# Silu and gating of the attention's four pairs of heads: in the attention's own gate units, or in the output stage

## The chip, the cores and the metric

One core of one Trainium2 chip. The metric is the device time of one launch in microseconds (us); each kernel is run several times and the median is taken. The profile is of one execution.

## What is computed

One layer of a backbone: 1024 tokens of width 1024 and 256 context tokens. A modulated RMS norm gives h; one projection gives eight groups of 512 columns; half of them feed a neighbourhood attention with 8 heads of 64, half a gated short convolution. Each branch is multiplied by the silu of its own gate column group, and one output projection and the residual follow. In the reference:

```python
q, k, v, za, u, bg, cg, zc = jnp.split(h @ w_in, SPLIT_POINTS, axis=-1)
attn = neighbourhood_attention(q, k, heads(v), kc, vc, rpb) * jax.nn.silu(za)
conv = gated_short_conv(u, bg, cg, zc, conv_w, conv_b)
x_new = x + gate[:, None] * (jnp.concatenate([attn, conv], axis=-1) @ w_out)
```

The change concerns the factor silu(za) and the division by the softmax's sums: attn = o * (1/sum) * silu(z), element by element, where o is the product of exponentials and v before it is divided.

## The kernel before, in words

Data stand with features on the 128 partitions and tokens along the free axis. Two heads make a pair: rows 0 to 63 are one head, rows 64 to 127 the other, so there are four pairs (NPAIR), numbered f = 0 to 3. The concatenated input of the output projection has eight such row blocks: 0 to 3 are the attention's pairs, 4 to 7 the convolution's groups. Every float32 product is made of three matmuls of high and low halves (`mm3`, lines 72 to 77).

There are four stages: (1) the norm and modulation of h, with the first convolution group; (2) the projections to q, k and v, which are stored to DRAM head by head; (3) the attention; (4) the output projection. What the change touches lies at the end of stage 2, in stage 3 and in stage 4.

**Stage 3** runs `quarter(n)` (line 1057) for n from 0 to 35: four quarters a head, and a pipeline over three of them (scores of quarter n, exponentials of quarter n-2, products with v of quarter n-3). Between these, on PE, run fillers: the remaining projections, one *unit* each (`unit`, line 338: 128 columns of w_in times all of h, in two halves of 512 tokens, 24 matmuls a half into PSUM tile `pu`, of which there are two). The fillers are first the four gate units of the attention (`attn_group(f)`, line 484), then the units of convolution groups 1 to 3 (`conv_group`, line 384). TICKS (line 33) says how many filler steps each quarter takes. PE, ACT, DVE and POOL run their instructions in the order in which this code writes them; transfers are placed by a scheduler that works with its own estimates of times.

What follows a unit on ACT and DVE is put into a list by `chore` (line 301); `do_acts` (line 307), at the end of each quarter, writes ACT's part. For a gate unit of the attention this is `silus` (line 477): both halves are put through silu from PSUM into `zs` (SBUF), and stored by SP's queue into DRAM tile `zs_d[f]`. The exponentials of the same stage need another table of ACT than silu does, so a table is loaded on either side.

At the end of each head, `finish` (line 1029) copies o and the sums (`ob`) and stores them from ACT's queue, `o_d` and `rs_d`. When a pair is done, `gated(p)` (line 1257) is started for pairs 0 to 2. It is a generator, and each quarter takes one step of it: load the sums, take reciprocals on DVE, store them (`ri_d`); then, for each half, load `zs` and `tb` (from o_d) and the reciprocals `rb` spread over 64 partitions each (`load_sums`, line 505, two transfers), all from SP's queue; multiply `zs` by `rb` on DVE; multiply `tb` by that on DVE and store it to `y_d[f]`. For pair 3 only the reciprocals are made (`recip`, line 498, from POOL's queue).

**Stage 4** takes the eight row blocks in the order FORDER = 4, 5, 6, 0, 1, 2, 3, 7. `put_y(f)` (line 1324) loads both halves of a block's y (tile `tb`, tag `zt`, four buffers, from ACT's queue), writes the high part on ACT (`yh`) and the low part on DVE (`yl`). For pair 3 it loads z's silu and o in place of y, the reciprocals from POOL's queue (tag `rb`, two buffers), and does the two multiplies on DVE there. `load_wo` (line 1315) loads and splits 128 rows of the output weights, one of two halves of 512 columns (`woraw`, two buffers; `woh` on ACT, `wol` on DVE). PE first runs all eight blocks through the first six of eight token tiles of the first half (the *first pass*), then the remaining ten tiles one after the other, 24 matmuls each. `out_tile` (line 1360) multiplies by the gate (DVE), adds x (POOL) and stores. In this stage no order is written by hand: the scheduler orders every engine's instructions by its own estimates.

The functions in full:

Of the kernel before, what the change touches and what calls it, by code (L numbers as in the profile page):

```python
# [10 lines left out]
F32 = mybir.dt.float32  # L11
F32R = mybir.dt.float32r
BF16 = mybir.dt.bfloat16
AF = mybir.ActivationFunctionType
ALU = mybir.AluOpType
# [4 lines left out]
P = 128  # L20
D = 1024
T = 1024
# [5 lines left out]
NPAIR = NH // 2  # L28
# [11 lines left out]
def body(tc, es, x, ctxt, w_ada, b_ada, w_in, q_g, k_g, rpbr, w_out, vecs, cst, out):  # L40
# [21 lines left out]
    pe, act, dve, pool = every = [ordered(e) for e in (nc.tensor, nc.scalar, nc.vector, nc.gpsimd)]  # L62
    sp = ordered(nc.sync)

    def sbuf(name, side=None, bufs=1):
        kw = {} if side is None else {"side": side}
        return tc.tile_pool(name=name, bufs=bufs, reuse_waits="tile", **kw)

    def psum(name):
        return tc.tile_pool(name=name, bufs=1, space=PSUM, reuse_waits="tile")  # L70
# [19 lines left out]
    def many(name, n, shape):  # L90
        return [dr.tile(shape, F32, name=f"{name}{i}")[:] for i in range(n)]
# [4 lines left out]
    o_d = many("o_d", NPAIR, [P, T])  # L96
    y_d = many("y_d", KT, [P, T])
    g_d = dr.tile([1, D], F32, name="g_d")
    rope_d = dr.tile([P, 2048], F32, name="rope_d")
    rs_d = many("rs_d", NPAIR, [2, 2, 512])  # L100
    zs_d = many("zs_d", NPAIR, [P, T])


    q_d = many("q_d", NH, [2, HD, 4, 2, 256])
# [46 lines left out]
    cvp = hs.enter_context(sbuf("cvp", side="right"))  # L151
# [149 lines left out]
    def chore(on_act=None, on_dve=None, queue=soon, frees=None):  # L301
        queue.append([on_act, on_dve, frees])
        if act not in strict:
            do_acts()
            do_dves()

    def do_acts():
        for c in soon + (slow if not any(c[1] and c[1].__name__ == "product" for c in soon) else []):
            if c[0]:
                c[0]()  # L310
                c[0] = None

    def do_dves(most=99):
        for queue in chores:
            while queue and not queue[0][0] and (queue is soon or most > 0 and not soon):
                on_dve = queue.pop(0)[1]
                if on_dve:
                    on_dve()
                    most -= 1
# [18 lines left out]
    def unit(col):  # L338

        w = ahead.pop(col, None)  # L340
        if w is None:
            w = []
            for r in loaded.pop(col, None) or unit_load(col):
                unit_split(r, w)
        nxt = follows.get(col)
        for half in range(2):
            cols = slice(half * 512, (half + 1) * 512)
            for k in range(KT):
                if k % 2 == 0:
                    yield None  # L350
                if k == 0:
                    while any(c[2] == half for c in slow):
                        do_acts()
                        do_dves()
                    ps = psm.tile([P, 512], F32, name="pu", tag="U", bufs=2)
                if k % 2 == 0:
                    tick = 4 * half + k // 2
                    if nxt and tick == 0:
                        raws = unit_load(nxt)
                    if nxt and tick in (3, 5):  # L360
                        unit_split(raws[tick // 5], ahead.setdefault(nxt, []))
                mm3(ps, *w[k], hh[k][:, cols], hl[k][:, cols], k == 0, k == KT - 1)
            yield half, ps

    def blocked(v):
        return v.rearrange("p (b r c) -> p b r c", b=4, r=16)
# [14 lines left out]
    def z_col(f):  # L381
        return CZA + f * P if f < 4 else CZC + (f - 4) * P
# [94 lines left out]
    def silus(z):  # L477
        out = []
        for half, ps in z:
            out.append(cvp.tile([P, 512], F32, name="zs", tag="ub", bufs=2))  # L480
            act.activation(out[half], ps, AF.Silu)
        return out

    def attn_group(f):

        z = []
        for got in unit(z_col(f)):
            if got:
                z.append(got)
            else:  # L490
                yield

        def on_act():
            for half, zs in enumerate(silus(z)):
                sp.dma_start(zs_d[f][:, half * 512:(half + 1) * 512], zs)
        chore(on_act)

    def recip(p, pl):

        ri = pl.tile([P, 16], F32, name="ri", tag="ri", bufs=4)  # L500
        pool.dma_start(ri, rs_d[p].rearrange("h b (x c) -> (h b x) c", c=16))
        dve.reciprocal(ri, ri)
        pool.dma_start(ri_d[p].rearrange("h (x c) -> (h x) c", c=16), ri)

    def load_sums(f, half, rb, queue):
        for i in range(2):
            queue.dma_start(rb[64 * i:64 * i + 64],
                            ri_d[f][i:i + 1, half * 512:(half + 1) * 512].broadcast_to([64, 512]))
# [390 lines left out]
    class gate_row:  # L899
# [7 lines left out]
        def load(self, kt):  # L907
            at, tag = ((bmp, "kc_s"), (uw, "uraw"))[kt % 2]
            self.w[kt] = [at.tile([P, 512], F32, name="gs", tag=tag, bufs=2) for _ in range(2)]
            for nh in range(2):  # L910
                sp.dma_start(self.w[kt][nh], w_ada[0, kt * P:(kt + 1) * P, 2 * D + nh * 512:2 * D + (nh + 1) * 512])
# [249 lines left out]
    for n in range(NT + 3):  # L1161


        p, t = divmod(n, NB)
# [89 lines left out]

    gating = []

    def gated(f):

        ri = ap.tile([P, 16], F32, name="ri", tag="ri", bufs=4)
        sp.dma_start(ri, rs_d[f].rearrange("h b (x c) -> (h b x) c", c=16))  # L1260
        yield
        dve.reciprocal(ri, ri)
        sp.dma_start(ri_d[f].rearrange("h (x c) -> (h x) c", c=16), ri)
        yield
        for half in range(2):
            cols = slice(half * 512, (half + 1) * 512)
            zs, tb, rb = (ap.tile([P, 512], F32, name=n, tag=n, bufs=1) for n in ("zs", "tb", "rb"))
            sp.dma_start(zs, zs_d[f][:, cols])
            sp.dma_start(tb, o_d[f][:, cols])
            load_sums(f, half, rb, sp)  # L1270
            yield
            dve.tensor_tensor(zs, zs, rb, ALU.mult)
            yield
            dve.tensor_tensor(tb, tb, zs, ALU.mult)
            sp.dma_start(y_d[f][:, cols], tb)

    with sbuf("att") as ap, psum("psb") as psb:
        sbank = psb.tile([P, 2, 512], F32, name="pss")
        strict[:] = every
        mx = ap.tile([P, T], F32, name="mx")  # L1280
        sb_new = lambda: ap.tile([P, 2, 384], F32, name="sb", tag="sb", bufs=3)
        mg = ap.tile([P, T], F32, name="mg")
        heads[0].load_v()
        for n in range(4 * NH + 4):
            h, g = divmod(n, 4)
            if 0 < h < NH and g == 0:
                heads[h].load_v()
            if h + 1 < NH and g:
                nx = heads[h + 1]
                for load in ((nx.masks, nx.load_q), (nx.load_k,), ())[g - 1]:  # L1290
                    load()
            quarter(n)
            if ready:
                p = ready.pop()
                if p < NPAIR - 1:
                    gating[:] = [gated(p)]
                else:
                    recip(p, ap)
        for _ in fill:
            do_dves()  # L1300
            do_acts()
        while soon or slow:
            do_dves()
            do_acts()
        strict[:] = []
# [5 lines left out]
    op = es.enter_context(sbuf("op"))  # L1311
# [12 lines left out]
    def put_y(yp, f):  # L1324

        yh = yp.tile([P, T], F32R, name=f"yh{f}")
        yl = yp.tile([P, T], F32R, name=f"yl{f}")
        for half in range(2):
            cols = slice(half * 512, (half + 1) * 512)
            tb = op.tile([P, 512], F32, name="tb", tag="zt", bufs=4)  # L1330
            if f == NPAIR - 1:
                zs = op.tile([P, 512], F32, name="zs", tag="zt", bufs=4)
                rb = op.tile([P, 512], F32, name="rb", tag="rb", bufs=2)
                act.dma_start(zs, zs_d[f][:, cols])
                act.dma_start(tb, o_d[f][:, cols])
                load_sums(f, half, rb, pool)
                dve.tensor_tensor(zs, zs, rb, ALU.mult)
                dve.tensor_tensor(tb, tb, zs, ALU.mult)
            else:
                act.dma_start(tb, y_d[f][:, cols])  # L1340
            tv = blocked(tb[:]) if f < NPAIR else by_row(tb[:])
            act.copy(natural(yh[:], half), tv)
            dve.tensor_tensor(natural(yl[:], half), tv, natural(yh[:].bitcast(F32), half), ALU.subtract)
        y[f] = yh, yl
# [32 lines left out]
    for n, (nh, t) in enumerate([(0, 6), (0, 7)] + [(1, t) for t in range(NB)]):  # L1377
        ps = bank("pout", "US"[n % 2])
# [54 lines left out]
```

## Time and profile before

| | |
|---|---|
| runs | 648.65, 649.57, 651.94 us; median 649.57 |
| profiled execution | 650.83 us, of which the span of the program's instructions is 649.0 |
| TensorE clock granted, mean | 0.992 |
| instructions | 10300 |
| DMA | 125.46 MB, 193 GB/s over the span |
| ACT busy | 322.6 us, 50% |

The profile names an instruction by engine, line, operation and the tiles it writes and reads (out<-in). Operations of stages 1 to 3 are written through one helper and all have line 55, so tiles tell them apart. PE is TensorE's matmuls, PEld its weight loads, DVE is VectorE, ACT ScalarE, POOL GpSimd, SP the engine that only issues transfers; a q behind an engine's name is its sequencer, such as ACTq issuing a transfer. A row of a timeline has the start and the length in us; in square brackets stands how long the engine idled before it and what released it. The first row of a pair `zs<-pu x2` may hold two instructions.

### The profile page before, as it was taken

The numbers are of one execution on the slowest core, as the hardware profiler recorded it, in microseconds if no ns is written. First come the engines' busy times: TensorE is split into PE (matmuls) and PEld (weight loads), VectorE is DVE, ScalarE is ACT, GpSimd is POOL, SyncE is SP. The second block draws the span as 40 slices with busy tenths as digits, with TensorE's granted clock in tenths as the row PEclk, the third lists the DMA queues.
The fourth block names the chain that finished last, engine by engine and source line by source line (L and its number), as shares of the span: only waits on it lengthen the run. The fifth ranks groups of instructions, "written<-read, shape, count | busy, mean of one in ns | idle before, by whom it ended". The sixth has DMA issues, their size and how long they took to land.

```text
span 649.0 us, 10300 instructions
## 1 busy us (share of the span) xinstructions
PE 631.6 (97%) x3482; PEld 542.1 (84%) x3482; DVE 431.1 (66%) x814; ACT 322.6 (50%) x693; POOL 130.1 (20%) x138
## 2 busy tenths in 40 slices
PE   7999999999999999999998999999999999999997
PEld 2577899999899999877787888888888888888885
DVE  1576756865775846458786789988998864575111
ACT  4566735533534544448676558565685644352000
POOL 2105003313223231102111111111211111004421
PEclk9799999999999999999999999999999999999999
DMA  8972656768694999799847677886862223865521
GB/s 322 321 250 97 166 177 197 212 223 232 214 288 139 270 269 237 196 238 216 215 126 195 152 171 195 208 213 155 229 168 75 74 77 115 310 236 204 197 102 49
DMA packets 118864, 125.46 MB, mean 193 GB/s; under 512 B 32817, under 2 KB 89353, under 8 KB 117532
## 3 DMA queue, kind: packets, MB, share of 16 engines
q1 hardware_dynamic: 112348, 113.23, 60.6%
q10 hardware_dynamic: 6208, 11.05, 5.4%
q8 instruction: 27, 0.44, 0.3%
q0 software_dynamic: 256, 0.54, 0.3%
q14 instruction: 25, 0.20, 0.1%
HBM read 88.01 MB, written 38.53 MB: 195 GB/s over the span
## 4 chain that ended last, share of the span: by engine, by line
PE 71%; DMA 9%; DVE 7%; ACT 5%; SPq 4%; issue 2%; POOL 1%; ACTq 0%; DVEq 0%
PE pu L55 20%; PE pacc L55 17%; PE po L55 5%; PE pout L76 4%; PE pout L75 4%; PE pout L74 4%; DMA k_s<-k_d 3%; SPq L55 3%; PE tr L55 3%; PE cacc L55 3%; PE pss L55 2%; PE acc L55 2%; PE pmx L55 2%; DVE mx L55 2%; DMA v<-v_d 2%
## 5 line engine op out<-in xcount | busy, mean ns | idle before, releaser
L55 PE MATMUL pu<-h,uh 128*128 128x512 f32 x544 | 169.0, 392 | 0.0
L55 PE MATMUL pacc<-wh,h 128*128 128x384 f32 x512 | 135.2, 338 | 0.0
L55 PEld LDWEIGHTS pu<-h,uh 128*128 128x128 f32 x544 | 98.2, 188 | 17.1
L55 PE MATMUL pu<-h,ul 128*128 128x512 f32 x272 | 106.3, 391 | 0.0
L55 PEld LDWEIGHTS pacc<-wh,h 128*128 128x128 f32 x512 | 92.8, 188 | 0.1
L55 POOL TENSOR_TENSOR plc<-sc,phc 128x512 fp32r<-128x512 f32 x32 | 42.7, 1335 | 224.1 <-ACT sc L55 88.5
L55 PE MATMUL pacc<-wl,h 128*128 128x384 f32 x256 | 85.6, 334 | 0.0
L55 POOL TENSOR_TENSOR ss<-ss,few 128x4 f32<-128x4 f32 (+1 forms) x40 | 42.0, 1051 | 127.1 <-DVE ss L55 126.7
L55 PEld LDWEIGHTS pu<-h,ul 128*128 128x128 f32 x272 | 51.1, 188 | 11.2
L55 DVE TENSOR_TENSOR mx<-mx,sb 128x384 f32<-128x384 f32 (+1 forms) x64 | 54.8, 864 | 2.0
L75 PE MATMUL pout<-wol,yh 128*128 128x512 f32 x128 | 49.8, 389 | 0.0
L76 PE MATMUL pout<-woh,yl 128*128 128x512 f32 x128 | 49.6, 389 | 0.0
L74 PE MATMUL pout<-woh,yh 128*128 128x512 f32 x128 | 48.3, 389 | 0.0
L55 PEld LDWEIGHTS pacc<-wl,h 128*128 128x128 f32 x256 | 48.1, 188 | 0.1
L55 DVE TENSOR_REDUCE ss<-sq 128x4 f32<-128x260 f32 (+1 forms) x40 | 15.7, 393 | 46.2 <-ACT sq L55 45.2
L55 ACT COPY mg<-pmx 128x256 f32<-128x256 f32 x32 | 12.0, 374 | 61.2 <-PE pmx L55 46.7
L55 ACT ACTIVATE sq<-pacc 128x256 f32<-128x256 f32 x32 | 12.3, 386 | 52.8 <-PE pacc L55 51.9
L1365 DVE TENSOR_TENSOR ot<-pout,gate 128x512 f32<-128x512 f32 x16 | 10.8, 687 | 38.6 <-PE pout L76 36.3
L55 DVE TENSOR_TENSOR pll<-sb,phl 128x768 fp32r<-128x768 f32 (+2 forms) x33 | 29.3, 889 | 8.9 <-ACT sb L55 8.9
L55 DVE TENSOR_TENSOR sc<-sc,mg 128x512 f32<-128x512 f32 x32 | 21.8, 682 | 18.4 <-ACT mg L55 18.4
L1366 POOL TENSOR_TENSOR ot<-ot,xr 128x512 f32<-128x512 f32 x15 | 20.1, 1347 | 68.2 <-DVE ot L1365 66.0
L55 ACT ACTIVATE qn<-pacc,ss 128x64 f32<-128x64 f32 x128 | 30.1, 330 | 6.5 <-POOL ss L55 3.2
(149 smaller groups left out, 1281.5 us busy)
## 6 DMA issues: line engine op xcount, KB each, us to landing
uraw<-in_w_in SPq DMA_DIRECT2D x34, 256.0 KB
q_d<-qs SPq DMA_DIRECT2D x64, 128.0 KB
k_s<-k_d SPq DMA_DIRECT2D x16, 512.0 KB
q_s<-q_d SPq DMA_DIRECT2D x32, 256.0 KB
wr<-in_w_in SPq DMA_DIRECT2D x40, 192.0 KB
slab<-in_w_ada SPq DMA_DIRECT2D x6, 1024.0 KB
t_d<-btw SPq DMA_DIRECT2D x8, 576.0 KB
bt<-t_d SPq DMA_DIRECT2D x8, 576.0 KB
```

The source lines that it names most:

```text
L55: i = emit(*a, **kw)
L74: i = pe.matmul(ps, ah, bh, start=first, stop=False)
L75: pe.matmul(ps, ah, bl, start=False, stop=False)
L76: pe.matmul(ps, al, bh, start=False, stop=last)
L1365: dve.tensor_tensor(ot, ps, gate[:, cols], ALU.mult)
L1366: (dve if (nh, t) == (1, NB - 1) else pool).tensor_tensor(ot, ot, xr, ALU.add)
```

## The change

The gate units of the attention no longer take silu. Each half of z is copied by ACT from PSUM as soon as it is done, and stored as it is (`z_d` in place of `zs_d`). `gated` shrinks to `inverse`: it still makes the reciprocals of pairs 0 to 2 in the attention, and nothing more. In `put_y` all four pairs are treated as pair 3 was: z and o are loaded from ACT's queue, the reciprocals from POOL's; silu is taken there on ACT, and the two multiplies are done there on DVE. Tag `zt` has six buffers in place of four.

```diff
     def attn_group(f):
 
-        z = []
+        def keep(half, ps):
+            z = cvp.tile([P, 512], F32, name="z", tag="ub", bufs=2)
+            act.copy(z, ps)
+            sp.dma_start(z_d[f][:, half * 512:(half + 1) * 512], z)
+
         for got in unit(z_col(f)):
             if got:
-                z.append(got)
+                chore(lambda got=got: keep(*got))
             else:
                 yield
-
-        def on_act():
-            for half, zs in enumerate(silus(z)):
-                sp.dma_start(zs_d[f][:, half * 512:(half + 1) * 512], zs)
-        chore(on_act)
...
-    def gated(f):
+    def inverse(f):
 
         ri = ap.tile([P, 16], F32, name="ri", tag="ri", bufs=4)
         sp.dma_start(ri, rs_d[f].rearrange("h b (x c) -> (h b x) c", c=16))
         yield
         dve.reciprocal(ri, ri)
         sp.dma_start(ri_d[f].rearrange("h (x c) -> (h x) c", c=16), ri)
-        yield
-        for half in range(2):
-            cols = slice(half * 512, (half + 1) * 512)
-            zs, tb, rb = (ap.tile([P, 512], F32, name=n, tag=n, bufs=1) for n in ("zs", "tb", "rb"))
-            sp.dma_start(zs, zs_d[f][:, cols])
-            sp.dma_start(tb, o_d[f][:, cols])
-            load_sums(f, half, rb, sp)
-            yield
-            dve.tensor_tensor(zs, zs, rb, ALU.mult)
-            yield
-            dve.tensor_tensor(tb, tb, zs, ALU.mult)
-            sp.dma_start(y_d[f][:, cols], tb)
...
-            tb = op.tile([P, 512], F32, name="tb", tag="zt", bufs=4)
-            if f == NPAIR - 1:
-                zs = op.tile([P, 512], F32, name="zs", tag="zt", bufs=4)
+            tb = op.tile([P, 512], F32, name="tb", tag="zt", bufs=6)
+            if f < NPAIR:
+                zs = op.tile([P, 512], F32, name="zs", tag="zt", bufs=6)
                 rb = op.tile([P, 512], F32, name="rb", tag="rb", bufs=2)
-                act.dma_start(zs, zs_d[f][:, cols])
+                act.dma_start(zs, z_d[f][:, cols])
                 act.dma_start(tb, o_d[f][:, cols])
                 load_sums(f, half, rb, pool)
+                act.activation(zs, zs, AF.Silu)
                 dve.tensor_tensor(zs, zs, rb, ALU.mult)
                 dve.tensor_tensor(tb, tb, zs, ALU.mult)
```

More of the change, by code (lines that the diff above doesn't have):

```diff
@@ L100, in body @@
     rs_d = many("rs_d", NPAIR, [2, 2, 512])
[L101 removed]
+    z_d = many("z_d", NPAIR, [P, T])
     q_d = many("q_d", NH, [2, HD, 4, 2, 256])
@@ L1295, in body @@
                 if p < NPAIR - 1:
-                    gating[:] = [gated(p)]
+                    gating[:] = [inverse(p)]
                 else:
```

## The prediction, made before the changed kernel ran

> **What bounds the kernel now.** The page's busy row comes first, then the table by stage, then PE's waits in the part that holds the edits.
>
> ```profile
> PE 631.6 (97%) x3482; PEld 542.1 (84%) x3482; DVE 431.1 (66%) x814; ACT 322.6 (50%) x693; POOL 130.1 (20%) x138
> ```
>
> PE works for 631.6 of 649.0 us. The change takes no matmul away, so it can win only PE's idle time, 17.4 us in all, and it loses whatever new idle time it makes. The table by stage says where that idle time lies (attention with its fillers runs from about 270 to 557, the output stage from 557 on):
>
> ```profile
> 270.00:350.00 80.00, 75.91 (x422) 62.78 (x422) 56.06 (x90) 50.24 (x83) 10.90 (x10) 1.00 0.83 205
> 350.00:450.00 100.00, 98.14 (x559) 83.79 (x558) 87.43 (x133) 62.28 (x105) 17.28 (x15) 0.98 0.73 180
> 450.00:542.00 92.00, 91.87 (x522) 77.87 (x521) 78.03 (x120) 55.81 (x92) 14.76 (x13) 1.00 0.43 122
> ```
>
> The columns are the stretch, its length, busy PE, PE loads, DVE, ACT, POOL, PE's clock, the DMA engines' share and GB/s. PE idles 4.1 us in 270 to 350, 1.9 in 350 to 450, 0.1 after that. The gating multiplies of pairs 0 to 2 run from 388 on, so they stand where PE hardly waits. What PE waited for (rows of its timeline, idle before and releaser in brackets):
>
> ```profile
> 300.79 0.33 PE L55 MATMUL pmx<-ci,mx 128*128 128x128 f32 x1 [0.65 <-DVE mx L55]
> 302.00 0.32 PE L55 MATMUL pmx<-ci,rm 128*128 128x128 f32 x1 [0.17 <-DVE rm L55]
> 324.33 0.33 PE L55 MATMUL po<-plc,v 128*65 128x256 f32 x1 [0.57 <-POOL plc L55]
> 325.21 0.32 PE L55 MATMUL pmx<-ci,rm 128*128 128x128 f32 x1 [0.19 <-DVE rm L55]
> 346.89 0.43 PE L55 MATMUL pmx<-ci,rm 128*128 128x128 f32 x2 [0.17 <-DVE rm L55]
> 355.18 0.30 PE L55 MATMUL pmx<-ci,mx 128*128 128x128 f32 x1 [1.51 <-DVE mx L55]
> 355.68 0.33 PE L55 MATMUL pmx<-ci,mx 128*128 128x128 f32 x1 [0.20 <-DVE mx L55]
> ```
>
> **Part 1: silu leaves the attention.** Behind each of these waits stands ACT. Its timeline at the places:
>
> ```profile
> 293.14 1.28 ACT L55 ACT_TABLE_LOAD   x1
> 294.44 1.09 ACT L55 ACTIVATE zs<-pu 128x512 f32<-128x512 f32 x2
> 295.41 0.38 ACT L55 COPY mg<-pmx 128x256 f32<-128x256 f32 x1
> 295.66 0.62 ACT L55 COPY sc<-pc 128x512 f32<-128x512 f32 x1
> 296.30 1.28 ACT L55 ACT_TABLE_LOAD   x1
> ...
> 319.88 1.28 ACT L55 ACT_TABLE_LOAD   x1
> 321.17 0.63 ACT L55 ACTIVATE phc<-sc 128x512 fp32r<-128x512 f32 x1
> ...
> 348.45 0.21 ACTq L1033 DMA_DIRECT2D rs_d<-ob  x1
> 350.17 0.45 ACTq L1034 DMA_DIRECT2D o_d<-ob  x1
> 350.72 0.37 ACT L55 COPY mg<-pmx 128x256 f32<-128x256 f32 x1 [4.74 <-PE po L55]
> ```
>
> A silu between two exps costs two table loads of 1.28 us. In the built program the loads around the silus of units 1, 2 and 3 are gone: six, 7.7 us of ACT time. The loads around the convolution's silus stay. The silus (0.55 each) become copies (sc at 295.66 has the same shape: 0.62), about as dear, and each half is copied when it is done. The gain is PE's waits, not ACT's 7.7 us.
> - At 300: mg at 295.41 stood behind a load and two silus, 2.4 us, and will stand behind one copy, 0.62: up to 1.7 us earlier. That covers 0.65 and 0.17.
> - At 324: phc comes 1.28 earlier, which covers 0.57 and 0.19. At 347 the same, 0.17. So far 1.75 us.
> - At 355: mg waits not for a table but for ACT's queue, which held o_d's issue until 350.17. In both programs a transfer on the ACT and SP queues is issued only when the one eight places before it has landed. For this o_d that was the second half of k_s; in the changed program, with one z store less behind k_s, it is the first half, for which rs_d, issued at 348.45, had waited before. So mg can come 1.7 us earlier. The bounds are nothing and the whole 1.71; I take 1.0, since k_s itself may land otherwise.
> Sum: 1.75 + 1.0 = 2.75 us, between 0.8 (if only the first wait goes) and 3.46 (all seven rows).
>
> The Trainium skill, "ScalarE: Activation LUTs", section "What ACT_TABLE_LOAD costs", gives about 1283 ns for a load and about 1380 ns more for a drain at each switch. The 1.28 of the rows agrees with the load; the instruction behind each starts within 0.02 us, so no drain shows and the measurement decides. By the page six switches would free 16.0 us instead of 7.7, but PE's waits would cap the gain all the same.
>
> **Part 2: gating leaves the attention.** Gone there are twelve DVE multiplies and 30 issues on SP's queue (per half: zs, tb, two rb, the store of y). Their rows:
>
> ```profile
> L55 DVE TENSOR_TENSOR zs<-zs,rb x6: 680/681/692, 388.1 to 529.1; 128x512 f32<-128x512 f32 x6
> L55 DVE TENSOR_TENSOR tb<-tb,zs x6: 679/682/686, 396.7 to 535.6; 128x512 f32<-128x512 f32 x6
> ```
>
> That is 8.2 us of DVE. It lies in 388 to 536, where PE idles next to nothing, so I count it at nothing; above, the bound is the 2.0 us that PE idles from 350 to 542 less the 1.71 already counted, 0.3. The reciprocals stay.
>
> **Part 3: the output stage.** Per half of pairs 0 to 2 it gains a load of z on ACT's queue, two loads of rb on POOL's, a silu on ACT and two multiplies on DVE; the load of y becomes one of o. The last pair gains its two silus. The answer for tile rb (min/median/max in ns, then the time from issue to landing), and the table by stage:
>
> ```profile
> L507 POOL DMA_DIRECT2D rb<-ri_d x4: 522/526/534, 550.9 to 552.5; - x4
> DMA to landing us min/median/max: 3.6/3.9/4.1
> ```
>
> ```profile
> 555.00:560.00 5.00, 5.00 (x24) 4.14 (x23) 2.29 (x4) 1.24 (x2) 0.00 (x0) 1.00 0.88 286
> 560.00:565.00 5.00, 5.00 (x24) 4.14 (x23) 2.23 (x4) 2.49 (x5) 0.00 (x0) 1.00 0.98 358
> 565.00:570.00 5.00, 5.00 (x23) 4.14 (x23) 2.60 (x5) 2.38 (x4) 0.00 (x0) 1.00 0.84 297
> 570.00:575.00 5.00, 5.00 (x23) 4.14 (x23) 4.12 (x7) 2.31 (x4) 0.00 (x0) 1.00 0.73 259
> 575.00:580.00 5.00, 5.00 (x23) 4.13 (x22) 3.43 (x6) 2.14 (x4) 0.00 (x0) 1.00 0.70 221
> 580.00:585.00 5.00, 5.00 (x23) 4.13 (x22) 3.28 (x5) 2.76 (x6) 0.00 (x0) 1.00 0.41 148
> ```
>
> ACT gains eight silus of 0.55 (half of the row at 294.44), 4.4 us, and DVE 12 x 0.68 = 8.2, in 555 to 585, where they are busy 13.3 and 18.0 of 30: both have room. The DMA engines gain 6 x 256 KB + 12 x 128 KB = 3.1 MB; at 300 to 358 GB/s that is 8.8 to 10.5 us of their time, and their idle share in these rows adds up to 7.3 us. So the last data of the first pass comes 2 to 3 us later than before.
>
> PE is the other side. It took up the first pass at the first row below, and 112 matmuls later the second tile of pair 3, 0.227 us each:
>
> ```profile
> 557.36 1.75 PE L74 MATMUL pout<-woh,yh 128*128 128x512 f32 x7
> ...
> 582.74 0.39 PE L74 MATMUL pout<-woh,yh 128*128 128x512 f32 x1
> ```
>
> In the built changed program PE's order is another: behind pair 0 stand nine matmuls of the seventh tile, then pair 1 with seven tiles, and around pairs 2 and 3 matmuls of the second half's first tile. Counted in matmuls, pair 0 comes at place 57, pair 1 at 84, pair 2 at 106, that tile's weights for y row 5 at 129, pair 3 at 133. On the old clock this is 570.3, 576.4, 581.4, 586.6 and 587.5; pair 3 has 5 us more time.
>
> Will the data be there? rb has two buffers, so a pair's rb is asked for only when the pair before has been multiplied. One round is the multiply 0.68, the second half's two issues (0.53 until the second) and 3.9 to land, with about 0.6 of other work on DVE: 5.7 us. Pair 0's multiplies need its loads:
>
> ```profile
> 555.25 0.43 ACTq L1340 DMA_DIRECT2D tb<-y_d  x1
> ...
> 564.14 0.62 ACT L1342 CAST yh<-tb 128x512 fp32r<-128x512 f32 x1 [1.73 <-DMA tb<-y_d]
> ```
>
> tb of pair 0 took 8.9 us in the full queues. Two more loads now stand before pair 0's second half, while y's row 6 is asked for some 3 us earlier (six zt buffers instead of four). I put pair 0's multiplies at 566.5; its low halves then follow at about 568, 2 us ahead of PE. Three rounds of 5.7 put pair 3's multiplies at 583.6. Behind that DVE has four more operations (2.5 us) until the split of row 5's weights is out: about 586.1 against 586.6. That is just in time. Below, the bound is no stall. Above, each round 1 us slower adds 3 us. I take 1.0.
>
> **The sum.** On the profiled execution: 650.83 - 2.75 + 1.0 = 649.1 us (its span is 649.0, 1.8 lie around it). That execution is 1.26 above the median of the runs, 649.57; the same step from the median gives 647.8.
>
> **The rivals.**
> 1. *Both sides turn out well.* All seven waits go, 3.46, and some tenths that the modelled matmul ends hide: 0.16 (0.389 in L74's rows of length, 0.227 of pace) at each of the five places, 0.8. The output stage hides everything. 649.57 - 4.3 = 645.3. For it speaks the new order on PE; against it the DMA share of 0.98.
> 2. *rb starves the first pass.* The twelve rb loads leave SP's queue for POOL's and run when the DMA engines are full. If they land in 7 us, not 3.9 (tb took 8.9 then), a round takes 8.8, three take 26.4, and pair 3 is 9.3 us later, so PE stands 8.8 us less the half microsecond of reserve. Taking 2.75 off gives 649.57 + 8.8 - 2.75 = 655.6. It decides from about 4.1 us to land, and is slower than before from 5.0. For it: three queues load at once around 560; against it: the row of 3.9 was measured at a share of 0.84 and POOL's queue holds only two loads at once.
> The Trainium skill, "SBUF — State Buffer", section "Who interferes with whom", says that a load issued from POOL waits for its descriptors while DVE runs an operation that holds their shared port, and gives 620 ns alone against 3100 beside it. It speaks against this change; by its extra 2.5 us a round the stall would be about 7, the time 653.8. The issues of 522 to 534 ns while DVE was busy show none of it.
> 3. *The attention's waits are the transfers'.* If the loads of k_s and v set when ACT goes on, PE waits as long whatever ACT does. Only the wait at 300 goes, 0.8, and the output costs 1.0: 649.8.
> 4. *It does not do what it says*: excluded, since the built order shows six table loads fewer and the silus in the output stage.
>
> **How the numbers follow.** My forecast (647.8) has 0.43, rival 1 0.22, rival 2 0.25, rival 3 0.10. 0.5% is 3.2 us, about what a measurement of this kernel can tell from no change. Faster is rival 1: 0.22. The forecast and rival 3 are within it: 0.53. Slower is rival 2: 0.25. The range goes from 644.9 (rival 1 with its small change) to 654.5, which takes in rival 2 up to a landing of 6.6 us, and leaves out its end.
>
> **What would show it.** Six ACT table loads fewer before 360. PE's waits in 290 to 360, 4.1 us in total before, at 1.5 or less. No y_d stores of pairs 0 to 2. In the first pass of the output, rb landing near 4 us, and PE waits of about 1 us in total, at the second half's weights or at pair 3. Wrong would be: PE waiting over 4 us there, with rb behind it (rival 2); o_d's issue held as long as before (rival 3); or new waits of PE between 360 and 542, which nothing here foresees.

## The result, and the profile after

The median of 15 runs is 652.3 us (650.07 to 654.26), beside 649.57 for the kernel before (15 runs, 647.52 to 652.62): ratio 1.0041, 95% interval 1.0027 to 1.0055. The kernel became 2.7 us slower, where 1.8 us faster had been forecast; the time lies in the range given. The profiled execution took 651.79 us.

The table by stage of the changed kernel (columns as in the prediction's table) shows both halves of it, a gain in the attention and a loss in the output stage:

```profile
270.00:350.00 80.00, 77.45 (x435) 64.70 (x434) 60.27 (x95) 45.78 (x83) 11.16 (x11) 1.00 0.82 208
350.00:450.00 100.00, 99.99 (x583) 85.98 (x582) 89.13 (x132) 63.31 (x107) 17.88 (x16) 1.00 0.64 156
450.00:542.00 92.00, 92.00 (x519) 78.35 (x518) 70.28 (x107) 55.27 (x91) 14.89 (x15) 1.00 0.32 81
542.00:560.00 18.00, 18.00 (x81) 14.92 (x80) 12.43 (x20) 7.27 (x12) 3.97 (x8) 1.00 1.02 342
560.00:600.00 40.00, 36.20 (x146) 28.92 (x145) 24.90 (x38) 16.42 (x28) 8.89 (x12) 0.91 0.73 223
```

The last two rows for the kernel before:

```profile
542.00:560.00 18.00, 18.00 (x82) 14.95 (x81) 8.58 (x14) 7.32 (x11) 3.40 (x6) 1.00 0.62 208
560.00:600.00 40.00, 40.00 (x179) 33.10 (x178) 23.83 (x36) 15.58 (x26) 6.78 (x5) 1.00 0.69 240
```

From 350 on in the attention PE hardly idles any more (99.99 of 100 us in the second row, 98.14 before). In 560 to 600 it idles 3.8 us, runs at a mean clock of 0.91, and does 146 matmuls in 40 us where it did 179. In 542 to 560 the DMA engines are full (1.02; 0.62 before).

To measure the two stages by themselves I take two rows that every kernel here has: PE's matmul on `rm` near 287 (`mx` and `rm` are maxima that DVE makes of the scores, and PE turns or spreads them), and the first matmul of the output stage. First the changed kernel, then the kernel before in a second profile (its first profile has them at 287.01 and 557.36):

```profile
287.67 0.43 PE L55 MATMUL pmx<-ci,rm 128*128 128x128 f32 x2 [0.52 <-DVE rm L55]
551.01 1.75 PE L74 MATMUL pout<-woh,yh 128*128 128x512 f32 x7
```

```profile
288.73 0.43 PE L55 MATMUL pmx<-ci,rm 128*128 128x128 f32 x2 [0.52 <-DVE rm L55]
556.41 1.75 PE L74 MATMUL pout<-woh,yh 128*128 128x512 f32 x7
```

From the first to the second row is the attention, called *Att* below; from the second to the end of the span is the output stage, *Out*:

| profile | Att, us | Out, us |
|---|---|---|
| before, three profiles | 270.35, 267.68, 268.19 | 91.64, 91.69, 91.69 |
| changed, two profiles | 263.34, 263.91 | 98.99, 97.77 |

So the attention gained about 5 us (263.6 against the mean of 268.7), and the output stage lost 6.1 to 7.3. The stage ahead of 287 differs by up to 3 us between profiles of one kernel, which is why the stages and not whole spans are compared below. Thirteen of the profiles in this study have the changed attention; their Att goes from 263.3 to 265.3, mean 264.2.

Where the output stage loses it, by rows of PE in the changed kernel:

```profile
571.20 0.50 PE L74 MATMUL pout<-woh,yh 128*128 128x512 f32 x1 [0.99 <-ACT yh L1330]
...
579.07 1.32 PE L74 MATMUL pout<-woh,yh 128*128 128x512 f32 x2 [2.81 <-ACT woh L1307]
580.19 0.63 PE L75 MATMUL pout<-wol,yh 128*128 128x512 f32 x1
580.62 0.63 PE L74 MATMUL pout<-woh,yh 128*128 128x512 f32 x1
581.04 0.63 PE L75 MATMUL pout<-wol,yh 128*128 128x512 f32 x1
```

PE waits 1.0 us for pair 1's high half, and 2.8 for the first weights of the second half. Behind that wait a matmul starts every 0.427 us in place of 0.227, for 14 matmuls: 2.8 us more, PE at about half its pace (in 560 to 600 its granted clock is 0.91 in the mean). Nothing in the prediction foresaw that.

### The profile page after: what moved, and what is told of

Same layout as the page of the kernel before. It is cut to its first block, busy times and chain, and to the rows that moved or that the text cites. A ratio compares the mean times of both kernels' runs of the same rounds, so it can differ in the third digit from the quotient of the medians.

```text
span 650.0 us, 10284 instructions
## 1 busy us (share of the span) xinstructions
PE 631.7 (97%) x3482; PEld 542.7 (83%) x3482; DVE 435.6 (67%) x814; ACT 318.9 (49%) x695; POOL 135.9 (21%) x150
## 4 chain that ended last, share of the span: by engine, by line
PE 73%; DMA 11%; DVE 5%; SPq 4%; ACT 3%; issue 2%; POOL 1%; ACTq 0%; DVEq 0%; POOLq 0%
PE pu L55 23%; PE pacc L55 17%; PE po L55 7%; PE pout L74 4%; PE pout L75 3%; PE pout L76 3%; SPq L55 3%; PE tr L55 3%; DMA k_s<-k_d 3%; PE cacc L55 3%; PE pss L55 3%; DMA woraw<-in_w_out 3%; PE pmx L55 2%; PE acc L55 2%; PE pc L55 2%; DMA tb<-y_d 2%
## 5 line engine op out<-in xcount | busy, mean ns | idle before, releaser
L55 DVE TENSOR_TENSOR mx<-mx,sb 128x384 f32<-128x384 f32 (+1 forms) x64 | 59.2, 933 | 2.0
L76 PE MATMUL pout<-woh,yl 128*128 128x512 f32 x128 | 46.4, 389 | 0.0
L74 PEld LDWEIGHTS pout<-woh,yh 128*128 128x128 f32 x128 | 25.1, 196 | 10.1 <-ACT woh L1307 3.2
L55 ACT COPY sc<-pc 128x512 f32<-128x512 f32 x32 | 18.8, 588 | 26.6 <-PE pc L55 26.6
```

Source lines behind the costliest of these rows:

```text
L55: i = emit(*a, **kw)
L74: i = pe.matmul(ps, ah, bh, start=first, stop=False)
L76: pe.matmul(ps, al, bh, start=False, stop=last)
```

## The experiments

Ratios are to the kernel before, with 95% intervals; Att and Out are from the profile; the kernel before has 267.7 to 270.4 and 91.7. An edit of a few lines lets the scheduler reorder the whole output stage, so small differences of Out are not read.

### Which part gives, which part takes

**Silu back in the gate units**, gating in the output stage:

```diff
-                chore(lambda got=got: keep(*got))
+                z.append(got)
...
-                act.activation(zs, zs, AF.Silu)
```

> The changed kernel, but the gate units take silu as they did before (with their six table loads), and the output stage only gates, with no silu. Theory A (the attention's gain of about 6.9 us comes from silu and its table loads leaving ACT; the output stage loses 7.2 to late loads): PE at the end of the attention within 1.5 us of the kernel before, the output stage loses 5 to 7 us as in the changed kernel, 655 to 657 us. Rival B (the attention gains because gating's transfers and multiplies leave it): PE is still 5 us or more ahead at 520, and the time is near the changed kernel's 652. Rival C (the eight silus on ACT are what makes the output late): the output loses 3 us or less, 650 to 652.

Measured 653.21 us, ratio 1.0063 (1.0045 to 1.0080); Att 265.9, Out 99.6. The time is lower than theory A's, and its account of the attention falls: with silu and its table loads in place the attention is still 1.8 to 4.5 us shorter than before. So gating's leaving seems worth more than the nothing that I gave it; a sharper measure stands below. Rival B's 5 us isn't reached either. Rival C falls clearly: without a single silu in the output stage it loses 7.9 us.

**Silu left out, gating in the attention as before:**

```diff
-            for half, zs in enumerate(silus(z)):
-                sp.dma_start(zs_d[f][:, half * 512:(half + 1) * 512], zs)
+            act.copy(z, ps)
+            sp.dma_start(zs_d[f][:, half * 512:(half + 1) * 512], z)
```

> The kernel before with one edit: the gate units copy z instead of taking silu, and nobody takes silu of it (left out). Gating stays in the attention, so the output stage is that of before. Theory A (table loads): the attention gains 5.5 to 7 us, the time is 642.5 to 644.5. Rival B (gating's transfers and multiplies gave a good part of the gain): the attention gains 3 us or less here, the time is 646.5 to 648. My prediction's 2.75 us for the first part would be 646.8.

646.84 us, ratio 0.9973 (0.9951 to 0.9996): 1.75 us by the ratio, between 0.3 and 3.2. Att is 267.95, Out 91.7. Theory A (5.5 to 7) falls; by the time, the prediction's first term, 2.75, lies in the interval. Its profile shows less: this Att is within those of the kernel before. The waits at 300, 302, 324 and 347 are gone, but ACT now stands behind o_d's issue at two places, and PE waits 1.24 us at the first of them and 1.30 at the second, near 356:

```profile
320.39 0.51 ACTq L1033 DMA_DIRECT2D o_d<-ob  x1
321.00 0.37 ACT L55 COPY mg<-pmx 128x256 f32<-128x256 f32 x1 [4.68 <-PE po L55]
...
325.48 0.30 PE L55 MATMUL pmx<-ci,mx 128*128 128x128 f32 x1 [1.24 <-DVE mx L55]
```

Table loads are seven here and in the changed kernel, as predicted, and thirteen before:

```profile
L55 ACT ACT_TABLE_LOAD x7 | 9.0, 1283 | 0.8 <-PEq L1404 0.7
```

**The reciprocals multiplied in the attention**, z and silu in the output stage:

```diff
+            dve.tensor_tensor(tb, tb, rb, ALU.mult)
+            sp.dma_start(y_d[f][:, cols], tb)
...
-                load_sums(f, half, rb, pool)
-                dve.tensor_tensor(zs, zs, rb, ALU.mult)
```

> The changed kernel, but pairs 0 to 2 are multiplied by the reciprocals in the attention, as before, with half of its DVE multiplies and most of its transfers; the output stage loads that product and z, takes silu and does one multiply. T2 (rb sets the first pass): the output loses 2 us or less, the attention keeps 6 us or more, 644 to 647. T1 (loads of z, silu on ACT and its order set it): waits of 2.5 us or more remain in the first pass, 649 to 653.

646.37 us, ratio 0.9959 (0.9946 to 0.9972); Att 264.8, Out 91.7. No wait of PE is left in the output stage: z's loads, all silus and one multiply a half fit in, as T2 says. What does not fit is rb, or the second multiply that comes with it; the next run tells which. The attention keeps 3.9 us of its gain, not the 6 that T2 names.

**No load of rb at all:**

```diff
-                load_sums(f, half, rb, pool)
-                dve.tensor_tensor(zs, zs, rb, ALU.mult)
+                dve.tensor_tensor(zs, zs, zs, ALU.mult)
```

> The changed kernel without any load of the spread reciprocals (zs is multiplied by itself in their place, so the division by the sums is left out); silu, both multiplies, and the loads of z and o stay. R1 (the loads of rb, with two buffers and landing 4 to 8 us after issue, set the first pass): no wait of PE over 0.3 us in the output stage, all of the attention's 7.0 us kept less 0.5, 644 to 646 us. R2 (it is the DVE multiplies, the silus or the loads of z and o): waits of 2 us or more remain, 648 to 652.

646.49 us, ratio 0.9957 (0.9937 to 0.9976); Att 263.9, Out 91.75, no wait. R1, half a microsecond above its range: all silus, both multiplies, z and o without rb cost the stage nothing.

### Why gating's leaving helps the attention

**The reciprocal's multiply on POOL**, an edit of the kernel that makes it in the attention:

```diff
-            dve.tensor_tensor(tb, tb, rb, ALU.mult)
+            pool.tensor_tensor(tb, tb, rb, ALU.mult)
```

> The kernel that multiplies by the reciprocals in the attention (646.4 us), with that multiply on POOL instead of DVE. D1 (the 1.4 us that this kernel gains less in the attention than the changed one, in pieces of 0.15 to 0.5 at quarters that hold a gating multiply, come from DVE's order ahead of mx and rm): PE at the end of the attention 6.5 to 7 us ahead, 645 us. D2 (they come from the transfers of the gating): no difference, 646.4, or slower by up to 1 us where POOL's subtractions wait behind the multiply.

650.0 us, ratio 0.9988 (0.9972 to 1.0005); Att 268.5, Out 91.7. Neither D1 nor D2: it lost 3.7 us in the attention. DVE's row beside POOL's multiply says why (this kernel, DVE and POOL; the same two operations of DVE take 2.18 in the kernel that it was made from):

```profile
389.43 3.17 DVE L55 TENSOR_TENSOR mx<-mx,sb 128x384 f32<-128x384 f32 x2
```

```profile
389.31 1.30 POOL L55 TENSOR_TENSOR plc<-sc,phc 128x512 fp32r<-128x512 f32 x1 [5.61 <-issue]
390.57 1.61 POOL L55 TENSOR_TENSOR tb<-tb,rb 128x512 f32<-128x512 f32 x1
```

The multiply left DVE's list and slowed DVE's maxima by 1 us instead, at the place where PE waits for them. One or both of the maxima run beside five of the six POOL multiplies. So this run doesn't test D1. What speaks for D1 are rows of the first two profiles. Before, DVE and then PE:

```profile
396.74 0.69 DVE L55 TENSOR_TENSOR tb<-tb,zs 128x512 f32<-128x512 f32 x1
...
399.93 1.48 DVE L55 TENSOR_TENSOR mx<-mx,sb 128x256 f32<-128x256 f32 x2
```

```profile
401.02 0.39 PE L55 MATMUL pu<-h,ul 128*128 128x512 f32 x1
401.55 0.41 PE L55 MATMUL pmx<-ci,mx 128*128 128x128 f32 x2
```

The same two matmuls in the changed kernel:

```profile
396.01 0.39 PE L55 MATMUL pu<-h,ul 128*128 128x512 f32 x1
396.25 0.38 PE L55 MATMUL pmx<-ci,mx 128*128 128x128 f32 x2
```

Before, 0.53 us lie between the two starts, after 0.24. A gating multiply of 0.69 stood ahead of mx on DVE, and PE waited 0.29 for mx. The view names no wait, because a matmul's row has a length of 0.39 and the next may start 0.227 after it: of 0.53 only 0.14 shows as idle. Five such places between 400 and 520 add up to 1.1 us. They are gone in the kernels without gating multiplies, and the largest are still there in the one that kept half of them.

How much gating's leaving is worth there can be read from a mark inside the attention, ahead of the first gating multiply (388): the eleventh group of matmuls on `rm`. Second profile of the kernel before, then the changed kernel:

```profile
364.30 0.41 PE L55 MATMUL pmx<-ci,rm 128*128 128x128 f32 x2
```

```profile
360.22 0.41 PE L55 MATMUL pmx<-ci,rm 128*128 128x128 f32 x2
```

From this mark to the first matmul of the output stage, the three profiles of the kernel before and the kernel without silu take 192.1 to 192.2 us, and the fourteen profiles without gating multiplies take 190.7 to 191.1, with or without silu in the gate units. So gating's leaving gives 1.3 us behind the mark, and DVE's order, by start times like those above, accounts for 1.1 of it. The kernel with half of the multiplies takes 191.9. No run takes the multiplies away and leaves the transfers, so the transfers' share isn't shown.

The larger part of the attention's gain lies ahead of the mark, where no gating multiply stands: 78.2, 75.6 and 76.0 us in the kernel before, 72.6 to 74.5 in the changed attention. Without silu alone it is 75.9, without gating alone 75.0. What shortens this part when both leave isn't shown.

### The two rb buffers

**Four buffers for rb:**

```diff
-                rb = op.tile([P, 512], F32, name="rb", tag="rb", bufs=2)
+                rb = op.tile([P, 512], F32, name="rb", tag="rb", bufs=4)
```

> The changed kernel with four buffers for the spread reciprocals rb instead of two (the last first-half weight tile moves to the other pool for the room). Theory T2 (the loop over two rb buffers sets the first pass): PE's waits of 1.0 and 2.8 us go or halve and the clock stays up, 646 to 648 us. Theory T1 (ACT's order and its queue of loads, with z, o and weights late in full DMA engines, set it; rb is late too but not last): waits of PE in the first pass stay above 2.5 us in sum, 650 to 653.

650.13 us, ratio 1.0010 (0.9993 to 1.0027); Att 264.4, Out 94.5, one wait of 1.8 at pair 1. (To make room, the last weight tile of the first half lies in the other pool.) Out's loss falls from between 6 and 7 to 2.8, so the buffers matter, but the time stays in T1's range, at its lower end.

**Eight buffers** (bufs=8; three weight tiles in the other pool):

> The changed kernel with eight buffers for rb, so that no load of it waits for a multiply (the first half's last three weight tiles move to the other pool for the room). The bytes are the same. L1 (the loop multiply, issue, landing over two buffers makes rb late): waits of PE in the output stage 0.5 us or less in sum, 645.5 to 647.5 us, as without rb. L2 (the DMA engines are full, the bytes of rb are what is too much): waits of 1.5 us or more remain, at rb or at whatever z, o or weights now come later, 648.5 to 651 us, as with four buffers (650.1).

651.92 us, ratio 1.0030 (1.0008 to 1.0052); Att 264.4, Out 97.5. L1 falls as it was put. All sixteen loads have landed by 564.2, yet PE waits 2.3 us for weights at 564.6 and 2.1 for pairs later: the rb loads now run ahead of what is needed first. More buffers are not better by themselves: Out is 3.0 longer than with four.

**rb from SP's queue:**

```diff
-                load_sums(f, half, rb, pool)
+                load_sums(f, half, rb, sp)
```

> The changed kernel with rb loaded from SP's queue instead of POOL's, two buffers as in it. R3 (POOL's queue is what makes rb land late): landing under 3.5 us, the output stage's loss falls to 3 us or less, 647 to 649 us. R4 (the DMA engines are full, whatever the queue, and now rb's loads also take places in the row of eight that z, o and the weights share): the waits stay or grow, 651 to 656 us.

651.05 us, ratio 1.0037 (1.0011 to 1.0063); Att 264.2, Out 96.6, three waits of 0.9 to 1.6. R4: POOL's queue isn't it.

### The half clock

**Thirteen matmuls in the long wait:**

```diff
+        for _ in range(13 if n == 2 else 0):
+            pe.matmul(ps, y[1][1][:, 7 * P:], wo[0, 1][0], start=True, stop=True)
```

> The changed kernel with thirteen matmuls more, whose results are overwritten, directly ahead of the second half's first matmul: PE works (13 x 0.227 = 2.95 us) where it waited 2.81 us. Theory C1 (the wait itself dropped PE's clock to half, 14 matmuls at 0.427 in place of 0.227, about 3.0 us): matmuls keep 0.227 behind it, the output stage loses 4 to 4.5 us instead of 7.3, the time is 649 to 650. Rival C2 (the clock falls for another reason at that place, such as load or time): the pitch of 0.427 remains, the time is 652 to 653.

The pitch stays at 0.227 behind them, as C1 says, but the time is 651.6 us, ratio 1.0038 (1.0019 to 1.0058), hardly better than the changed kernel; Out is 97.1. PE waits 0.6 for the same weights behind the thirteen, and 0.65 for a low half seven us later. One profile doesn't settle C1, since the changed kernel's second profile, below, keeps 0.227 behind a wait too. There Out is 1.2 shorter than in the first, not 2.8: the half clock spent more than half of its time on data that were late anyway.

**A ladder of idle times:**

```diff
+            d = rp.tile([P, P], F32R, name=f"d{n}")
+            dve.tensor_copy(d, last[:, :P])
+            for _ in range((1, 3, 5, 7, 10, 14)[n - 4]):
+                dve.tensor_tensor(d, d[:].bitcast(F32), d[:].bitcast(F32), ALU.subtract)
+            pe.matmul(ps, d, wo[1, 4][0], start=True, stop=True)
```

> The changed kernel with a chain of 2, 4, 6, 8, 11 and 15 small DVE operations ahead of the last six output tiles, on which PE waits, and one matmul more a tile: idle times of PE that grow from about 0.7 to about 4 us in one program, 24 matmuls behind each. If an idle time of 1.5 to 2.8 us drops the clock (as the traces of both kernels suggest), the pitch is 0.227 behind the shortest and 0.427 for 12 or more matmuls behind all from about 1.5 us on. If a longer one is needed (3.4 us), only the last one or two show it.

690.09 us in one run. The shortest step came out at 2.3 us of idle, not 0.7, and the longest at 6.6. Behind each of the six the pitch is 0.427 for 6 to 13 matmuls or so; the first of them:

```profile
614.30 0.50 PE L1372 MATMUL pout<-woh,d 128*128 128x512 f32 x1 [2.33 <-DVE d L1371]
614.64 0.48 PE L74 MATMUL pout<-woh,yh 128*128 128x512 f32 x1
614.91 0.63 PE L75 MATMUL pout<-wol,yh 128*128 128x512 f32 x1
615.34 0.63 PE L76 MATMUL pout<-woh,yl 128*128 128x512 f32 x1
```

### The same kernels again

> The kernel before once more, for a second profile. If its profile shows the wait of 1.5 us near 355 with about 1.5 us of slow clock behind it again, these belong to the kernel; if it shows the wait and no slow clock, the clock's part is chance, and the attention's gain over a usual execution is about 5.5 and not 7 us.

> The kernel before a third time, for its profile. If its attention agrees with the second profile within 0.5 us (2.7 less than the first from 285 us on, no slow clock behind the wait near 355), the first profile was the unusual one, and the changed kernel's gain in the attention is 3.8 to 4.4 us and not 7.

They took 649.9 and 649.8 us, and differ by 0.5 us in Att and not at all in Out. Neither shows a slow pitch behind 355. In the first profile it cost about 1.4 us (matmuls of `pss` 0.320 apart in place of 0.175), so that profile was the unusual one.

> The changed kernel once more, for a second profile. If the three parts of the output stage's loss (1.1 at pair 1, 3.1 at the second half's first weights, 3.0 of half clock) come back within 0.5 us each, the first profile may stand for the kernel; if not, only their sum.

650.0 us. The waits come back: 0.8 at pair 1, 3.1 at the second half's weights, and one of 1.0 more for their low half; the half clock does not, though the wait was longer. So at these lengths the clock falls in one execution and not in another; the waits belong to the kernel.

### What else makes the data late

**z's loads left out**, the rb loop as it is:

```diff
-                act.dma_start(zs, z_d[f][:, cols])
-                act.activation(zs, zs, AF.Silu)
+                act.activation(zs, tb, AF.Silu)
```

> The changed kernel without the loads of z (silu is taken of o in its place, so z is left out); rb keeps its two buffers, its loads from POOL's queue and both multiplies. L2 (the DMA engines are full for 40 us, and about 2 MB more or less decide): with 2.1 MB less PE waits 0.5 us or less in the output stage, 645 to 647.5 us, as without rb. L1 (the loop over two rb buffers makes y late): the waits at pair 1 and at the second half's weights remain 2 us or more, 649 to 652.

650.45 us, ratio 1.0005 (0.9987 to 1.0023); Att 264.8, Out 96.1. L2 falls: 2.1 MB fewer, a DMA share of 0.71 from 560 to 580 (0.98 in the changed kernel), rb landing after 3.6 us in the median, and still a loss of 4.4. Its ACT shows a second thing:

```profile
561.24 0.63 ACT L1323 ACTIVATE zs<-tb 128x512 f32<-128x512 f32 x1 [1.39 <-DMA tb<-o_d]
561.25 0.33 ACTq L1321 DMA_DIRECT2D tb<-o_d  x1
```

ACT waits 1.39 us for one load of o, and in the moment when it goes on, the next load of o is issued. The load stood behind the silu in ACT's order. While ACT waits for data it asks for none.

**Both edits** (no z, eight rb buffers):

> The changed kernel with both edits at once: eight buffers for rb, and no loads of z (silu of o in its place, z left out). Theory T (two limits lie close together, the loop over two rb buffers and the full DMA engines; each alone is enough for a loss of 4 to 6 us, which is why neither edit alone helped): waits of PE in the output stage 0.7 us or less, 645 to 647.5 us. Rival (a third thing, ACT's order or the six buffers of z and o, keeps y late): waits of 2 us or more, 649 to 652.

657.37 us, ratio 1.0104 (1.0067 to 1.0142); Att 263.9, Out 101.5. Theory T falls, the rival stands: with rb at hand and the DMA engines at a share of 0.48 to 0.64 from 566 on, PE waits 4.4 us for pair 1, since o's loads still go out one at a time behind ACT's waits.

**The second half's weights last:**

```diff
+        if nh:
+            act.copy(raw[:, :1], y[7][0][:, :1].bitcast(F32))
```

> The changed kernel, but the second half's weights are loaded only when the last block's y (row block 7) is made: each load waits for a copy of one column of that tile into its buffer. W1 (the wait of 3.1 to 3.6 us belongs to these weights alone, which PE's order puts ahead of pairs 2 and 3): it goes, and nothing as long takes its place; 647.5 to 649.5 us. W2 (everything loaded in the stage is late by that much): the next data in PE's order, pair 2's y, is waited for instead, or the second half's weights still are, later; 650.5 to 654.

652.25 us, ratio 1.0035 (1.0016 to 1.0053); Att 263.7, Out 99.5. W2: the wait moves to pair 2's y, 3.2 us.

**The loads from SP's queue:**

```diff
-        act.dma_start(raw, w_out[0, f * P:(f + 1) * P, nh * 512:(nh + 1) * 512])
+        sp.dma_start(raw, w_out[0, f * P:(f + 1) * P, nh * 512:(nh + 1) * 512])
...
-                act.dma_start(zs, z_d[f][:, cols])
-                act.dma_start(tb, o_d[f][:, cols])
+                sp.dma_start(zs, z_d[f][:, cols])
+                sp.dma_start(tb, o_d[f][:, cols])
...
-                act.dma_start(tb, y_d[f][:, cols])
+                sp.dma_start(tb, y_d[f][:, cols])
```

> The changed kernel with its loads of y, z, o and of the output weights issued from SP's queue instead of ACT's; rb stays on POOL's queue with two buffers. Theory A (ACT issues the next loads in its program order, so while it waits for one load's data, in front of a silu, a cast or a copy, it can't ask for the next): waits of PE in the output stage fall from 4.5 us or so to 2 or less, 647 to 649 us. Theory B (rb's two buffers and the filled DMA engines set it, whoever issues): waits of 3 us or more, 650.5 to 653.

651.06 us, ratio 1.0020 (0.9998 to 1.0041); Att 263.8, Out 97.3. PE waits 3.1 us for the second half's weights. By itself that is theory B.

**Both: SP's loads and four rb buffers:**

> As the run with SP's loads, and four buffers for rb (with the last first-half weight tile in the other pool, as in the run with four buffers alone, which gave 650.1 us). If ACT's order and rb's buffers each hold the loads back, both edits together leave PE waits of 1 us or less in the output stage, 645.5 to 647.5 us. If the bytes in the full DMA engines are the end of it, waits of 2 us or more remain, 649 to 651, as with four buffers alone.

646.33 us, ratio 0.9937 (0.9915 to 0.9959); Att 264.7, Out 92.3. It beats both kernels, by 3.6 us and by 6.0. PE works through the output stage with the DMA engines fuller than in the kernel before (its shares are 0.62 and 0.69):

```profile
542.00:560.00 18.00, 18.00 (x81) 14.92 (x80) 14.78 (x24) 7.62 (x15) 6.75 (x13) 1.00 0.83 272
560.00:600.00 40.00, 39.98 (x175) 32.46 (x174) 24.93 (x38) 15.44 (x26) 8.60 (x9) 1.00 0.78 240
```

The bytes are those of the changed kernel, and rb lands no sooner (5.9 us in the median). So the bytes by themselves don't make the loss. Two orders of asking make it: rb asked for only when a multiply has freed one of two buffers, and z, o and weights asked for by an engine that waits for data itself. Each alone still costs 2.8 (ACT's order, four buffers) or 5.6 (two buffers, SP's loads); together 6 to 7; with both gone 0.6. ACT's order costs nothing where no rb is loaded (Out 91.75 in that run), so it hurts only beside rb's loads.

## Why the prediction was wrong, point by point

- **Part 1, the silus, 2.75 us: the size is within its bounds, the mechanism is shown only in part.** Six table loads went, and the waits of its seven rows all went in the changed kernel (PE's waits in 290 to 360 add up to 0.6 us, 4.1 before). But the copy of z in place of silu alone gave 1.75 (0.3 to 3.2), and in its profile the waits behind the table loads went while o_d's issue held ACT at 320 and 351, for waits of 1.24 and 1.30. The step "I take 1.0" at 355 has no run of its own: that wait varied by 1.5 us among the three profiles of the kernel before.
- **Part 2, "so I count it at nothing; above, the bound is ... 0.3": wrong.** Behind 365 gating's leaving gave 1.3 us. The step took PE's idle time from busy columns. Matmul rows of 0.39 at a pitch of 0.227 cover waits of up to 0.16, and DVE's order made five waits that hardly show there: 1.1 us, in the start times. Ahead of 365 the attention gained more than either edit gives alone, and why stays open.
- **Part 3, "I take 1.0": wrong by 5 to 6 us, and it decided the sign.** The sub-step that failed is "One round is ... 5.7 us": the changed kernel's second multiplies of the four pairs stand 10.3, 8.3 and 7.1 us apart, and rb took 5.5 to land, not 3.9:

```profile
L506 POOL DMA_DIRECT2D rb<-ri_d x16: 516/522/534, 541.9 to 576.4; - x16
DMA to landing us min/median/max: 4.0/5.5/8.0
```

```profile
559.03 0.69 DVE L1326 TENSOR_TENSOR tb<-tb,zs 128x512 f32<-128x512 f32 x1
...
569.28 0.69 DVE L1326 TENSOR_TENSOR tb<-tb,zs 128x512 f32<-128x512 f32 x1
...
577.56 0.69 DVE L1326 TENSOR_TENSOR tb<-tb,zs 128x512 f32<-128x512 f32 x1
...
584.62 0.69 DVE L1326 TENSOR_TENSOR tb<-tb,zs 128x512 f32<-128x512 f32 x1
```

  The last of them, 584.6, is only 1.0 us behind the 583.6 that I forecast for pair 3, but that is chance. The old clock has to go from both sides: PE began the stage at 551.0 and not at 557.4, and pair 0 came with it. Counted from PE's first matmul of the stage, pair 0 was forecast at 9.1 us and came at 8.0; the three rounds were to take 17.1 and took 25.6; so pair 3 came at 33.6 in place of 26.2, 7.4 us late against a reserve of 0.5. The stage lost 7.3 in this profile, though PE stood still earlier in its order, at pair 1 and at the second half's weights.
  Of the 8.5 us that the rounds took too long, rb's landing explains 3 x 1.6 = 4.8 (an estimate from its median). The round has more in it than rb. ACT's silu waits behind other work and behind issues that wait for a place in the row of eight:

```profile
561.96 0.33 ACTq L1321 DMA_DIRECT2D zs<-z_d  x1
562.33 0.62 ACT L1307 CAST woh<-woraw 128x512 fp32r<-128x512 f32 x1 [1.42 <-DMA y_d<-cv]
...
564.15 0.63 ACT L1324 ACTIVATE zs<-zs 128x512 f32<-128x512 f32 x1 [1.20 <-DVE wol L1308]
```

  The cast of the weights at 562.33 stands behind the issue at 561.96, and that waited for a store that SP had issued at 553.47. That ACT's own issues hold up its work I had seen at 355 ("ACT's queue ... held o_d's issue"), and didn't carry over to the output stage.
- **Rival 1 (0.22)** was right for the attention, where its seven waits went and hidden ones too; the output stage hid next to nothing.
- **Rival 2 (0.25) had the stage and the sign.** With the 5.5 us that rb took to land, its own sum gives 649.57 + 3 x 1.6 - 0.5 - 2.75 = 651.1; 652.3 came. Its account is a part of the cause: four buffers alone left 2.8 us of the loss. That the time lies in the range is rival 2's doing; the forecast's sum missed on both sides, 2.3 us too little gain in the attention and 5 to 6 too little loss behind it. Rival 3 falls for the changed kernel, where the waits at 324 and 355 went too; without silu alone, ACT was held by o_d's issue much as it says.
- **The Trainium skill's rule** weighed with rival 2 ("SBUF — State Buffer", "Who interferes with whom": a load from POOL waits for descriptors while DVE holds the port) isn't the cause: with rb loaded from SP's queue the stage still loses about 5 us (Out 96.6). That section also says that a probe saw `tensor_copy` stall a load and `tensor_tensor` not, and in this stage DVE runs almost nothing but TENSOR_TENSOR, so the rule hardly bore on it.

## What to carry to other kernels

When an earlier stage gets faster, the deadlines of the next stage and its first loads both move: count each from the start of that stage, not on the old clock. A load is late when it is asked for late: look at what stands in front of its issue, a buffer that a multiply must free or a compute instruction of the same engine that waits for another load, and expect that removing one of two such holds shows only a part until the other goes too. Read small waits of PE from start to start, not from busy shares, and take a second profile before explaining 1 or 2 us; a mark inside a stage can part what varies from run to run (here ahead of 365) from what doesn't.

## What the runs showed of the hardware

- **Half clock after short idle.** Idle times of 2.3 to 6.6 us in the ladder dropped PE to a pitch of 0.427 each time, for 6 to 13 matmuls or so. Elsewhere it went both ways: the pitch fell behind 1.5 us (the kernel before, first profile), 1.8 (silu back in the units), 2.8 (the changed kernel), 3.1 (the loads from SP's queue) and 3.2 (the second half's weights last), and stayed behind 1.8 (four rb buffers), 2.3 (eight rb buffers, and no z) and 3.1 (the changed kernel, second profile). The Trainium skill, "TensorE: Matmul & The Clock Gate", Part 1, tells of a free-running window of about 3.4 us and a fall after an idle window; that the same wait did it in one run and not in the next would fit a window that runs freely, but idle times well under 3.4 us were enough here.
- **POOL and DVE.** DVE's maxima, two inputs in SBUF, took 3.17 us beside a POOL multiply and 2.18 without. The Trainium skill's "SBUF — State Buffer", "Who interferes with whom", says that a DVE instruction with two SBUF inputs contends with a POOL instruction that reads SBUF; the row agrees.
